# Part of the feed-forward weights prepared during the mixers, through DRAM scratch

## The chip, the cores and the metric

The kernel runs on one core of a Trainium2 chip. The metric is device time in microseconds. The core has five engines that run side by side, each in its own order: TensorE (PE in the profile, with its weight loads as PEld), VectorE (DVE), ScalarE (ACT), GpSimd (POOL) and SyncE (SP), whose queue (SPq) issues all DMAs here.

## The reference

One inference step of a trunk of two layers over 640 tokens (512 latent, 128 context), width 1024. Each layer normalises and modulates x, projects it once, feeds three token mixers (A: grouped-query attention, B: latent attention, C: a gated DeltaNet scan), merges them behind sigmoid gates, and runs a SwiGLU feed-forward of width 2816:

```python
def trunk_layer(x, cvec, p, ctx, angs):
    ...
    h = rms_norm(x, p['norm1']) * (1 + sc1) + sh1
    mix, new_ctx = mixer_block(h, p, ctx, angs)
    x = x + g1 * mix
    h = rms_norm(x, p['norm2']) * (1 + sc2) + sh2
    x = x + g2 * ((jax.nn.silu(h @ p['w_gate']) * (h @ p['w_up'])) @ p['w_down'])
    return x, new_ctx
```

All weights and inputs are float32.

## The kernel before

**Float32 by parts.** A float32 operand is split into a float16 high part and a float16 low part (`split`: ScalarE writes the high part, VectorE the low part). `mm3` multiplies two such operands with three matmuls per 128 rows of depth: low weight with high input, high with high, high with low input. Weights are split in the kernel, as they come in from DRAM.

**A layer.** `layer` writes the program in this order: input projection, mixer C's short convolution and triangular solve, mixer A's projections and attention, with the scan of mixer C (`ds` on PE) run step by step between them; then mixer B; then `merge`; then `ffn`. The rest of the input projection (`background`, gates and other columns, PSUM tile `f` from `hh`) has a very low priority and fills PE wherever nothing else is ready; `bgload` converts its weights. The triangular solve is a chain of products `zw` and differences `z` on VectorE; the first scan step needs its end. A scheduler sets each engine's order from priorities and a modelled time line; each engine then runs its list in order.

**The feed-forward.** Gate, up and down products are done with a Strassen-like scheme of 7 products instead of 8 on 2 × 2 quarters. `block` runs the 7 products of one output block. A weight chunk is a 512 KB tile `wf` of 4 quarters. `lhs_parts` turns it into 7 left operands: three quarters are split directly (tiles `wh`, `wl` for the first chunk of a block, `uh`, `ul` for the second), four sums of quarters go into `ls` (three on GpSimd, one on VectorE) and are split into `vh`, `vl`:

```python
            self.split(w[0], w[1], a[:, 1:4], SW)
            tt = lambda i, x, y, op: (nc.gpsimd if i in SUMP else nc.vector).tensor_tensor(t[:, i], x, y, op=op)
            tt(0, a[:, 0], a[:, 3], ALU.add)
            ...
            self.split(v[0], v[1], t, SW)
```

`wf` and `ls` have two buffers each, shared by all chunks in turn.

`gate_up(u)`, u = 0 to 10, runs two blocks (g: gate, up) of two chunks each (c), 44 chunks per layer. ScalarE copies intermediate products out of PSUM (`du2`, `du3`, `dp1`: `du` and `dp` in the profile), VectorE adds, GpSimd multiplies gate and up (`ff_s`). `inputs(u)` then makes the input of the down product: four differences `ts` on GpSimd, split by ScalarE and VectorE into `f`. `down` runs over units 0 to 3 after unit 4's gate and up, over 4 to 7 after unit 8's, and over 8 to 10 at the end; it reads another 24 chunks, 4 of them of half size, so 22 full ones. That makes 66 blocks of weights per layer. During layer 0's feed-forward PE also computes layer 1's modulations (`wm`).

## Time and profile before

| | us |
|---|---|
| median of 3 runs (lowest, highest) | 2723.09 (2721.92, 2725.84) |
| the profiled execution | 2721.82 |
| its span in the trace | 2719.8 |
| layer 0: solve, scan, mixer B | 250 to 338, 338 to 632, 632 to 785 |
| layer 0: feed-forward, gate and up of units 0 to 4, then 5 to 8 | 913 to 1068, 1118 to 1232 |
| layer 1: feed-forward, gate and up of units 0 to 4, then 5 to 8 | 2262 to 2400, 2446 to 2556 |

The stretches are read from the trace by which line PE works for, to a few us. Busy time is the time in which an engine executes; a wait row names the engine and line that waited, what its wait ended with, and the sum, number and longest of these waits. "Clock" is the granted TensorE clock as a share of full speed.

### The profile page before, as it was taken

The page shows a single profiled execution, that of the slowest core. Times are in us where ns is not written, and L with a number is a line of the kernel's source. Part 1 is how long each engine was busy: PE and PEld are TensorE (multiplying, and loading weights), DVE is VectorE, ACT ScalarE, POOL GpSimd, SP SyncE. Part 2 cuts the span into 40 slices and gives each one's busy share as a digit, 9 for nine tenths or more (in the row PEclk, how much of TensorE's full clock was granted, in tenths as well). Part 3 has the DMA queues.
Part 4 walks back from the last instruction along what each step waited for, and adds up shares of the span by engine and source line. Part 5 has one row for each costly group of instructions (what it writes and reads, how often), then busy time and mean ns, then how long its engine had stood idle before and what let it go on. Part 6 is the DMA issues. An engine that isn't in the chain of part 4 may idle for free.

```text
span 2719.8 us, 52951 instructions
## 1 busy us (share of the span) xinstructions
PE 2495.5 (92%) x21022; PEld 1613.9 (59%) x21022; DVE 1810.2 (67%) x2966; ACT 1295.5 (48%) x2466; POOL 1093.1 (40%) x1012
## 2 busy tenths in 40 slices
PE   5999999999998899999889989999989988889896
PEld 3656666566345656656566666665653565656574
DVE  5749854325756778878787497442277657888887
ACT  5532754444642544444465346554545444444444
POOL 3252111111137567565533632011112565766764
PEclk9999999999998999999989999999999999999998
DMA  7787564436434164432243965543462621222222
GB/s 295 225 260 233 151 195 124 126 123 202 114 131 157 61 206 131 162 117 89 73 137 106 264 184 161 163 122 119 126 205 74 210 78 40 78 78 78 78 82 67
DMA packets 249400, 382.50 MB, mean 141 GB/s; under 512 B 109824, under 2 KB 155968, under 8 KB 249152
## 3 DMA queue, kind: packets, MB, share of 16 engines
q1 hardware_dynamic: 249152, 379.12, 45.0%
q8 instruction: 165, 2.70, 0.4%
q14 instruction: 83, 0.68, 0.1%
HBM read 291.30 MB, written 73.92 MB: 134 GB/s over the span
## 4 chain that ended last, share of the span: by engine, by line
PE 44%; DVE 18%; POOL 14%; DMA 12%; issue 5%; ACT 5%; SPq 2%; DVEq 0%; POOLq 0%; ACTq 0%
PE f L195 12%; PE g L195 8%; POOL ls L1210 8%; PE ao L872 5%; PE s L195 5%; DMA wf<-in_w_gu 3%; POOL ts L1191 3%; DMA wf<-in_w_down 2%; DVE wl L183 2%; POOL ff_s L1307 1%; DVE vl L189 1%; DVE wl L189 1%; DVE ul L189 1%; DVE z L671 1%; ACT wh L188 1%
## 5 line engine op out<-in xcount | busy, mean ns | idle before, releaser
L195 PEld LDWEIGHTS <-wh 128*128 128x128 f16 x5760 | 560.1, 99 | 250.8 <-issue 34.8
L195 PEld LDWEIGHTS <-wl 128*128 128x128 f16 x2880 | 285.6, 99 | 176.9 <-issue 70.8
L195 PE MATMUL s<-xs,vh 128*128 128x320 f16 x1408 | 308.2, 302 | 25.3 <-ACT du L213 10.7
L195 PEld LDWEIGHTS <-vh 128*128 128x128 f16 x2112 | 209.9, 100 | 92.1 <-issue 5.3
L195 PE MATMUL f<-hh,wh 128*128 128x320 f16 x896 | 251.1, 302 | 1.7 <-ACT st L213 1.6
L195 PE MATMUL f<-hh,wl 128*128 128x320 f16 x896 | 251.2, 301 | 0.0
L1210 POOL TENSOR_TENSOR ls<-wf 128x256 f32<-128x256 f32 (+1 forms) x136 | 137.3, 1014 | 203.7 <-DVE vl L189 188.4
L875 POOL TENSOR_TENSOR pacc<-pe,pacc 128x512 f32<-128x512 f32 x64 | 84.2, 1315 | 325.7 <-ACT pe L213 315.5
L195 PE MATMUL s<-xs,vl 128*128 128x320 f16 x704 | 203.9, 302 | 0.2 <-DVE vl L189 0.2
L195 PE MATMUL g<-hh,wh 128*128 128x320 f16 x704 | 198.7, 304 | 2.8 <-ACT sq L213 1.5
L195 PE MATMUL g<-hh,wl 128*128 128x320 f16 x704 | 198.4, 304 | 0.0
L189 DVE SCALAR_TENSOR_TENSOR vl<-ls,vh 128x1024 f16<-128x1024 f32 (+1 forms) x136 | 185.7, 1389 | 10.8 <-ACT vh L188 10.8
L329 DVE SCALAR_TENSOR_TENSOR wl<-wf,wh 128x512 f16<-128x512 f32 x130 | 89.1, 713 | 137.2 <-ACT wh L213 136.8
L195 PE MATMUL s<-f,vh 128*128 128x320 f16 x704 | 159.9, 310 | 17.1 <-ACT du L213 9.3
L195 PEld LDWEIGHTS <-vl 128*128 128x128 f16 x1056 | 104.8, 99 | 95.8 <-issue 49.2
L183 DVE SCALAR_TENSOR_TENSOR wl<-wf,wh 128x1024 f16<-128x1024 f32 (+4 forms) x116 | 132.6, 1157 | 33.3 <-ACT wh L182 33.0
L188 ACT ACTIVATE vh<-ls 128x1024 f16<-128x1024 f32 (+1 forms) x136 | 133.8, 1020 | 39.4 <-POOL ls L1210 39.3
L195 PE MATMUL f<-hl,wh 128*128 128x320 f16 x896 | 148.7, 299 | 0.0
L195 PE MATMUL s<-xs,wh 128*128 128x320 f16 x528 | 133.6, 306 | 10.0 <-ACT du L213 10.0
L814 POOL TENSOR_TENSOR rc<-rc,rot 128x512 f32<-128x512 f32 (+1 forms) x16 | 27.6, 1724 | 283.3 <-DVE rc L813 266.9
L182 ACT ACTIVATE wh<-wf 128x1024 f16<-128x1024 f32 (+4 forms) x116 | 95.2, 832 | 92.3 <-PE g L195 72.9
L195 PE MATMUL s<-xs,uh 128*128 128x320 f16 x528 | 134.4, 305 | 4.2 <-ACT uh L188 4.2
(382 smaller groups left out, 6202.1 us busy)
## 6 DMA issues: line engine op xcount, KB each, us to landing
wm<-in_w_mod SPq DMA_DIRECT2D x96, 512.0 KB, 4.6
wf<-in_w_gu SPq DMA_DIRECT2D x88, 512.0 KB, 3.6
wf<-in_w_in SPq DMA_DIRECT2D x112, 256.0 KB, 3.5
wf<-in_w_in SPq DMA_DIRECT2D x44, 512.0 KB, 4.0
wf<-in_w_down SPq DMA_DIRECT2D x40, 512.0 KB, 3.6
d_s<-sd SPq DMA_DIRECT2D x20, 768.0 KB, 5.4
d_gate<-st SPq DMA_DIRECT2D x96, 160.0 KB, 3.1
sd<-d_s SPq DMA_DIRECT2D x20, 768.0 KB, 5.7
```

The costliest lines, as they stand in the source:

```text
L182: nc.scalar.activation(wh, wf, AF.Copy, scale=SW)
L183: nc.vector.scalar_tensor_tensor(wl, wf, SW, wh, op0=ALU.mult, op1=ALU.subtract)
L188: nc.scalar.activation(hi, src, AF.Copy, scale=scale)
L189: nc.vector.scalar_tensor_tensor(lo, src, scale, hi, op0=ALU.mult, op1=ALU.subtract)
L195: mm = lambda *a, **k: nc.tensor.matmul(out, *a, skip_group_check=more, **k)
L329: nc.vector.scalar_tensor_tensor(wl[:, sl], wf, SW, wh[:, sl], op0=ALU.mult, op1=ALU.subtract)
L671: nc.vector.tensor_tensor(z[a, j + 1:N, 0:cc], z[a, j + 1:N, 0:cc], wj, op=ALU.subtract)
L814: nc.gpsimd.tensor_tensor(w[:n], w[:n], self.rot[:n, NS:], op=ALU.mult)
L872: nc.tensor.matmul(po[64 * j:64 * j + 64, :], vt(h, kt), es[j], start=n == 0, stop=n == 4)
L875: nc.gpsimd.tensor_tensor(acc[1], es[1], acc[1], op=ALU.add)
L1191: sub = lambda i, x, y: (self.nc.gpsimd if i in pool else self.nc.vector).tensor_tensor(out[:, i], x, y, op=ALU.subtract)
L1210: tt = lambda i, x, y, op: (nc.gpsimd if i in SUMP else nc.vector).tensor_tensor(t[:, i], x, y, op=op)
```

## The change

Eighteen chunks per layer are converted before the feed-forward: the second chunk (c = 1) of both blocks of units 1 to 5 while mixer A runs, and of units 6 to 9 while mixer B runs. `prepare` loads each in two halves of 256 KB (`pf`), makes the sums (`pt`) and the split parts (`pp`), and stores the half's 7 + 7 parts in a scratch tile in DRAM, `d_pw`, 448 KB per half. All this has a priority below the background projection, and one buffer of each tile. In the feed-forward, `lhs` takes such a chunk with one load of 896 KB and no work on any other engine. Other chunks go as before, but all 14 parts of a chunk now lie in one tile `pw` with five buffers, in place of `wh`/`wl`, `uh`/`ul` and `vh`/`vl`. The weights are laid out in another order in DRAM, so that halves of a chunk are contiguous. `wh` and `wl` of the other weights move to a pool that is closed before the feed-forward.

```diff
+AT7 = {1: 0, 2: 1, 4: 2, 5: 3, 6: 4, 7: 5, 3: 6}
+PWB = 5
+READY = ([(u, g, 1) for u in range(1, 6) for g in range(2)], [(u, g, 1) for u in range(6, 10) for g in range(2)])
...
-        self.wp = pool("wst", 3)
+        self.wp = pool("wst", 2)
...
-        wh = self.sb(pool or self.wp, [128, n], "wh", F16)
-        wl = self.sb(pool or self.wp, [128, n], "wl", F16)
+        wh = self.sb(pool or self.wq, [128, n], "wh", F16)
+        wl = self.sb(pool or self.wq, [128, n], "wl", F16)
...
-    def lhs_parts(self, pool, src, n, c):
-
-        nc = self.nc
-        wide = lambda p, tag, dt, bufs: self.sb(p, [128, 1024], tag, dt, bufs)[:, :4 * n].rearrange("p (q n) -> p q n", q=4)
+    def lhs_parts(self, out, a, t):
+        nc = self.nc
+        self.split(out[:, :, 0, 0:3], out[:, :, 1, 0:3], a[:, :, 1:4], SW)
+        tt = lambda i, x, y, op: (nc.gpsimd if i in SUMP else nc.vector).tensor_tensor(t[:, :, i], x, y, op=op)
+        tt(0, a[:, :, 0], a[:, :, 3], ALU.add)
+        tt(1, t[:, :, 0], a[:, :, 1], ALU.subtract)
+        tt(2, a[:, :, 1], a[:, :, 0], ALU.subtract)
+        tt(3, a[:, :, 2], t[:, :, 1], ALU.subtract)
+        self.split(out[:, :, 0, 3:7], out[:, :, 1, 3:7], t, SW)
+    def lhs(self, pool, src, n, ready=None):
+        nc = self.nc
+        tile = lambda p, tag, bufs, dt=F32, q=4: self.sb(p, [128, q * 256], tag, dt, bufs)[:, :q * 128 * n]
         with self.tc.high_priority():
-            a, t = wide(self.wp, "wf", F32, 2), wide(pool, "ls", F32, 2)
-            nc.sync.dma_start(a, src)
-            if c % 2:
-                w = [self.sb(pool, [128, 768], tag, F16, 2)[:, :3 * n].rearrange("p (q n) -> p q n", q=3) for tag in ("uh", "ul")]
-            else:
-                w = [wide(self.wp, tag, F16, None)[:, 1:4] for tag in ("wh", "wl")]
-            v = [wide(pool, tag, F16, 4) for tag in ("vh", "vl")]
-            self.split(w[0], w[1], a[:, 1:4], SW)
-            tt = lambda i, x, y, op: (nc.gpsimd if i in SUMP else nc.vector).tensor_tensor(t[:, i], x, y, op=op)
-            tt(0, a[:, 0], a[:, 3], ALU.add)
-            tt(1, t[:, 0], a[:, 1], ALU.subtract)
-            tt(2, a[:, 1], a[:, 0], ALU.subtract)
-            tt(3, a[:, 2], t[:, 1], ALU.subtract)
-            self.split(v[0], v[1], t, SW)
-        pick = lambda x, q: [x[i][:, q] for i in range(2)]
-        return {1: pick(w, 0), 2: pick(w, 1), 4: pick(w, 2), 5: pick(v, 0), 6: pick(v, 1), 7: pick(v, 2), 3: pick(v, 3)}
+            out = tile(pool, "pw", PWB, F16, 14)
+            if ready is not None:
+                nc.sync.dma_start(out, ready)
+            out = out.rearrange("p (n i q c) -> p n i q c", n=n, i=2, q=7)
+            if ready is None:
+                quads = lambda x: x.rearrange("p (n q c) -> p n q c", n=n, q=4)
+                a, t = tile(self.wp, "wf", 2), tile(pool, "ls", 2)
+                nc.sync.dma_start(a, src)
+                self.lhs_parts(out, quads(a), quads(t))
+        return {q: [[out[:, k, i, j] for k in range(n)] for i in range(2)] for q, j in AT7.items()}
+    def prepare(self, l, pool, parts):
+        nc = self.nc
+        with self.tc.high_priority(-2 * 10 ** 6):
+            for u, g, c in parts:
+                d = self.d_pw[u, g, c] = self.sb(self.dp, [128, 2, 14 * 128], f"d_pw{l}{u}{g}{c}", F16)
+                for k in range(2):
+                    a, t = self.sb(pool, [128, 1, 4, 128], "pf"), self.sb(pool, [128, 1, 4, 128], "pt")
+                    o = self.sb(pool, [128, 1, 2, 7, 128], "pp", F16)
+                    nc.sync.dma_start(a.rearrange("p n q c -> p (n q c)"), self.a["w_gu"][l, u, g, c, :, 512 * k:512 * k + 512])
+                    self.lhs_parts(o, a, t)
+                    nc.sync.dma_start(d[:, k], o.rearrange("p n i q c -> p (n i q c)"))
...
-                self.mm3(bank, lambda k, i: w[q][i][:, 128 * k:128 * k + 128], lambda k, i: rhs(q, i, k0 + k), n,
+                self.mm3(bank, lambda k, i: w[q][i][k], lambda k, i: rhs(q, i, k0 + k), n,
...
-                chunks = [(self.lhs_parts(wp, self.a["w_gu"][l, u, g, c], 256, c), 2 * c, 2) for c in range(2)]
+                chunks = []
+                for c in range(2):
+                    ready = self.d_pw.get((u, g, c))
+                    if ready is not None:
+                        ready = ready.rearrange("p k x -> p (k x)")
+                    chunks.append((self.lhs(wp, self.a["w_gu"][l, u, g, c], 2, ready), 2 * c, 2))
...
-                    src = self.a["w_down"][l, m // 2][:, 512 * u:512 * (u + n)].rearrange("p (q n) -> p q n", q=4)
-                    chunks.append((self.lhs_parts(wp, src, 128 * n, len(chunks)), u, n))
+                    chunks.append((self.lhs(wp, self.a["w_down"][l, m // 2][:, 512 * u:512 * (u + n)], n), u, n))
...
+        self.d_pw = {}
+        self.wq = self.pool(ws, f"wst{l}", 3)
...
+            self.prepare(l, self.pool(e1, f"pa{l}"), READY[0])
...
+            self.prepare(l, self.pool(es, f"pb{l}"), READY[1])
...
-    r["w_gu"] = quads(gu).reshape(L, NF // 2, 2, 2, 128, 4, 256)
+    r["w_gu"] = quads(gu).swapaxes(-3, -2).reshape(L, NF // 2, 2, 2, 128, 1024)
```

GpSimd, one unit of gate and up in layer 1's feed-forward. `ff_s` is gate times up, `ts` the differences for the down product, `ls` the weight sums. Before:

```order
L1307 TENSOR_TENSOR ff_s<-ff_s,ff_o 128x320 x2
L1191 TENSOR_TENSOR ts<-ff_s 128x320 x2
L1191 TENSOR_TENSOR ts<-ff_s,ts 128x320
L1210 TENSOR_TENSOR ls<-wf 128x256 x2
L1191 TENSOR_TENSOR ts<-ff_s,ts 128x320
L1210 TENSOR_TENSOR ls<-ls,wf 128x256 x2
L1307 TENSOR_TENSOR ff_s<-ff_s,ff_o 128x320
L1210 TENSOR_TENSOR ls<-wf,ls 128x256 x2
L1210 TENSOR_TENSOR ls<-wf 128x256
L1210 TENSOR_TENSOR ls<-ls,wf 128x256
L1210 TENSOR_TENSOR ls<-wf 128x256
L1210 TENSOR_TENSOR ls<-wf,ls 128x256
```

After:

```order
L1331 TENSOR_TENSOR ff_s<-ff_s,ff_o 128x320 x2
L1196 TENSOR_TENSOR ts<-ff_s 128x320 x2
L1196 TENSOR_TENSOR ts<-ff_s,ts 128x320
L1207 TENSOR_TENSOR ls<-wf 128x2x128
L1196 TENSOR_TENSOR ts<-ff_s,ts 128x320
L1207 TENSOR_TENSOR ls<-ls,wf 128x2x128
L1207 TENSOR_TENSOR ls<-wf,ls 128x2x128
L1331 TENSOR_TENSOR ff_s<-ff_s,ff_o 128x320
L1207 TENSOR_TENSOR ls<-wf 128x2x128
L1207 TENSOR_TENSOR ls<-ls,wf 128x2x128
L1207 TENSOR_TENSOR ls<-wf,ls 128x2x128
```

Before, twelve `ls` of a unit (two more follow the rows shown) stand between one group of `ff_s` and the next; after, six.

VectorE at the end of layer 0's triangular solve (`zw`, `z`), with mixer A's rotation (`rc`, `aq`) between. `pf`, `pt` and `pp` are the tiles of `prepare`. Before:

```order
L669 TENSOR_TENSOR zw<-lt,z 64x87
L813 STREAM_SHUFFLE rc<-aq 128x512
L671 TENSOR_TENSOR z<-z,zw 64x3x29
L815 TENSOR_TENSOR aq<-aq,rot 128x512
L669 TENSOR_TENSOR zw<-lt,z 64x60
L671 TENSOR_TENSOR z<-z,zw 64x2x30
L669 TENSOR_TENSOR zw<-lt,z 64x31
L816 TENSOR_TENSOR aq<-aq,rc 128x512
L671 TENSOR_TENSOR z<-z,zw 64x31
```

After:

```order
L1207 TENSOR_TENSOR pt<-pf 128x128
L674 TENSOR_TENSOR zw<-lt,z 64x87
L194 SCALAR_TENSOR_TENSOR aql<-aq,aqh 128x640
L676 TENSOR_TENSOR z<-z,zw 64x3x29
L194 SCALAR_TENSOR_TENSOR pp<-pf,pp 128x384
L674 TENSOR_TENSOR zw<-lt,z 64x60
L194 SCALAR_TENSOR_TENSOR pp<-pt,pp 128x512
L676 TENSOR_TENSOR z<-z,zw 64x2x30
L188 SCALAR_TENSOR_TENSOR wl<-wf,wh 128x256
L674 TENSOR_TENSOR zw<-lt,z 64x31
L676 TENSOR_TENSOR z<-z,zw 64x31
```

Rows of `prepare` now stand between the last steps of the chain. From the first `zw` to the last `z` of this layer VectorE has 266 rows before and 332 after, 36 of them of `prepare`: 12 of the 20 halves of this stretch.

PE after the last scan step of layer 0 (`ds`). `f` from `hh` is the background projection; `f` and `ao` from `yh` is the next branch's output projection. Before:

```order
L759 MATMUL ds<-sd,S 64x64 x2
L761 MATMUL ds<-sd,sw 64x64 x2
L195 LDWEIGHTS wl
L195 MATMUL f<-hh,wl 128x320
L195 LDWEIGHTS wh
L195 MATMUL f<-hh,wh 128x320
```

After:

```order
L764 MATMUL ds<-sd,S 64x64 x2
L766 MATMUL ds<-sd,sw 64x64 x2
L200 LDWEIGHTS wh
L200 MATMUL f<-yh_5056,wh 128x320
L200 LDWEIGHTS wh
L200 MATMUL ao<-yh_5056,wh 128x320
L200 LDWEIGHTS wl
L200 MATMUL f<-yh_5056,wl 128x320
```

Before, 187 matmuls of the background projection stand behind the last `ds` matmul (205 in layer 1); after, none.

## Rows read from the trace of the kernel before

**Rows 1.** Page, part 1: busy us (share of span) and instructions of each engine.

```profile
PE 2495.5 (92%) x21022; PEld 1613.9 (59%) x21022; DVE 1810.2 (67%) x2966; ACT 1295.5 (48%) x2466; POOL 1093.1 (40%) x1012
```

**Rows 2.** Stretches: length, PE, PEld, DVE, ACT, POOL busy, clock, DMA share, GB/s.

```profile
250.00:338.00 88.00, 81.14 (x795) 57.61 (x794) 82.21 (x202) 56.20 (x108) 15.30 (x17) 1.00 0.58 160
338.00:632.00 294.00, 291.11 (x3440) 186.94 (x3439) 109.74 (x178) 146.63 (x311) 39.75 (x32) 1.00 0.47 138
632.00:785.00 153.00, 146.53 (x741) 65.79 (x741) 99.68 (x176) 80.99 (x173) 28.93 (x21) 1.00 0.44 133
913.00:1068.00 155.00, 141.84 (x1101) 87.91 (x1101) 117.34 (x163) 69.65 (x117) 95.49 (x97) 0.98 0.50 167
...
1118.00:1232.00 114.00, 105.22 (x800) 67.95 (x798) 88.56 (x115) 49.38 (x81) 72.67 (x70) 0.97 0.42 144
...
2262.00:2400.00 138.00, 122.59 (x828) 82.74 (x828) 107.88 (x135) 63.43 (x103) 92.03 (x85) 0.95 0.21 66
...
2446.00:2556.00 110.00, 97.25 (x691) 67.56 (x690) 89.06 (x108) 50.26 (x83) 75.71 (x72) 0.98 0.25 79
...
2608.00:2656.00 48.00, 46.05 (x339) 32.83 (x337) 39.07 (x54) 24.09 (x38) 30.46 (x30) 1.00 0.27 78
```

**Rows 3.** PE waits (us, times, longest): 913:1068, 1118:1232, 2262:2400, 2446:2556, 2262:2705 in turn.

```profile
PE s L195 <- ACT du L213: 4.5, 2, 2.4
...
PE s L195 <- ACT du L213: 4.4, 3, 2.5
...
PE s L195 <- DVE ul L189: 1.8, 1, 1.8
...
PE s L195 <- ACT du L213: 7.7, 6, 2.0
PE s L195 <- ACT uh L188: 4.0, 2, 2.1
...
PE s L195 <- DVE ul L189: 1.6, 4, 0.5
...
PE s L195 <- DVE ul L189: 4.8, 3, 1.8
PE s L195 <- ACT du L213: 3.8, 3, 1.8
PE s L195 <- DVE ff_s L1236: 3.6, 3, 1.4
...
PE s L195 <- DVE ul L189: 10.7, 11, 3.2
PE s L195 <- ACT uh L188: 6.2, 5, 2.1
```

**Rows 4.** Waits of GpSimd and ScalarE, 2262 to 2400.

```profile
POOL ls L1210 <- DVE vl L189: 28.4, 5, 6.7
...
ACT f L188 <- POOL ts L1191: 26.6, 8, 5.7
```

**Rows 5.** Chain that ended last, 2465 to 2535: start us, us, what.

```profile
2473.25 3.65 DMA wf<-in_w_gu
...
2501.56 3.61 DMA wf<-in_w_gu
```

**Rows 6.** Conversion operations: count, ns min/median/max, first and last start, forms.

```profile
L1210 DVE TENSOR_TENSOR ls<-wf x136: 412/943/1082, 831.2 to 2690.6; 128x256 f32<-128x256 f32 x128, 128x128 f32<-128x128 f32 x8
...
L1210 POOL TENSOR_TENSOR ls<-wf,ls x136: 584/790/1704, 836.1 to 2691.6; 128x256 f32<-128x256 f32 x128, 128x128 f32<-128x128 f32 x8
...
L189 DVE SCALAR_TENSOR_TENSOR vl<-ls,vh x136: 678/1219/1892, 838.6 to 2695.5; 128x1024 f16<-128x1024 f32 x128, 128x512 f16<-128x512 f32 x8
...
L189 DVE SCALAR_TENSOR_TENSOR ul<-wf,uh x68: 551/951/1608, 839.9 to 2689.1; 128x768 f16<-128x768 f32 x60, 128x384 f16<-128x384 f32 x8
```

**Rows 7.** The attention's running sum on VectorE, same columns.

```profile
L874 DVE TENSOR_TENSOR pacc<-pe,pacc x64: 678/692/1645, 464.8 to 2120.4; 128x512 f32<-128x512 f32 x64
```

**Rows 8.** DMA issues: count, KB each, median us to landing.

```profile
sd<-d_s SPq DMA_DIRECT2D x20, 768.0 KB, 5.7
```

More of the change, by code (lines that the diff above doesn't have):

```diff
@@ L1418, in layer @@
         tc = self.tc
-        ys = ExitStack()
+        ys, ws = ExitStack(), ExitStack()
         self.yh, self.yl = [], []
+        self.d_pw = {}
+        self.wq = self.pool(ws, f"wst{l}", 3)
         def branch(b):
@@ L1511, in layer @@
                 self.branch_out(l, 2, bgp)
+        ws.close()
         wr = self.pool(ys, f"wr{l}", 4, "right")
@@ L1577, in layout @@
     quads = lambda w: np.stack([w[..., 1, 0, :, :], w[..., 0, 0, :, :], w[..., 0, 1, :, :], w[..., 1, 1, :, :]], -3)
-    r["w_gu"] = quads(gu).reshape(L, NF // 2, 2, 2, 128, 4, 256)
+    r["w_gu"] = quads(gu).swapaxes(-3, -2).reshape(L, NF // 2, 2, 2, 128, 1024)
     dn = f("w_down").reshape(L, 2, NF // 2, 128, 4, 2, 128).transpose(0, 4, 3, 5, 1, 2, 6)
-    dn = quads(dn)
-    r["w_down"] = cat([dn[..., u:u + 2, :].reshape(L, 4, 128, -1) for u in range(0, NF // 2, 2)], -1)
+    r["w_down"] = quads(dn).swapaxes(-3, -2).reshape(L, 4, 128, -1)
     return {k: np.ascontiguousarray(v) for k, v in r.items()}
```

## Prediction

> **What bounds the kernel now.** I read the engines' busy time first [rows 1]. TensorE (PE) is busy 92% of the span of 2719.8 us, so no change can bring much unless it gives PE back some of the other 8%. The next view is the table of stretches [rows 2]. Its columns are length, then busy time of PE, weight loads, VectorE, ScalarE and GpSimd, then the granted clock. While layer 0's DeltaNet scan runs (338 to 632), PE is busy 291.11 of 294 us. In mixer B (632 to 785) it is busy 146.53 of 153. In the gate and up parts of the feed-forward it is busy less: 141.84 of 155 and 105.22 of 114 in layer 0, 122.59 of 138 and 97.25 of 110 in layer 1. This is where the lost time is.
>
> Matmul counts say the same. The stretch 2608 to 2656 is fully fed at clock 1.00: 46.05 us for 339 matmuls, or 0.136 us each [rows 2]. The 828 matmuls of 2262 to 2400 would need 112.6 us at that price and take 138. The 691 of 2446 to 2556 would need 94 and take 110.
>
> Why PE waits there is in its waits [rows 3]. Some end on `ul` and `uh`, the low and high halves of the second weight chunk of a block. More end on `du`, a copy from PSUM by ScalarE. That copy is short, so it is late because of what stands in front of it. On ScalarE that is `f`, which waited 26.6 us in this stretch for `ts`, GpSimd's sums [rows 4]. On GpSimd the sums `ls` of the weight chunks waited 28.4 us for `vl`, the split that frees the `ls` buffer [rows 4]. GpSimd runs in order, so `ts` stands behind those `ls`. A ring of load, split, sum, split and next load thus runs through four engines. The chain of what ended last shows its period: two of its load steps, one unit of gate and up apart, start 28.31 us from each other [rows 5]. A unit has 168 matmuls (7 products, 3 matmuls per k, 4 k, 2 blocks), or 22.8 us at 0.136. **The conversion ring, not PE, sets the pace of gate and up.**
>
> **Removed from the feed-forward.** In units 1 to 9 of each layer the second chunk of both blocks arrives converted: 18 of 44 chunks. Each takes with it the `ul` split (0.95 us median), the fourth sum (0.94) and the `vl` split (1.22) on VectorE, 3.1 us together, and three sums of about 0.79, 2.4 us, on GpSimd [rows 6]. A unit keeps two of four conversions, so the ring's part of the period falls from 28.3 to about half, 14 to 15 us, well under PE's 22.8. The sums' order on GpSimd shows it: six `ls` per unit instead of twelve around the same `ts`.
>
> What PE gets back, for both layers:
> - `ul` and `uh` in the gate and up stretches: 1.8 + 1.6 + 4.8 + 4.0 = 12.2 us [rows 3]. These tiles belong to the chunk that is now ready. I take 12.
> - `du`, with the two sums that wait behind it: 4.5 + 4.4 + 7.7 + 3.8 + 3.6 = 24.0 us [rows 3]. `ts` still comes from GpSimd, still waits for the gate and up values, and units 0 and 10 change nothing. I take 15, bounds 6 and 22.
> - The clock. The granted clock was 0.98, 0.97, 0.95 and 0.98 in those four stretches [rows 2], a loss of 3.1 + 3.4 + 6.9 + 2.2 = 15.6 us. It stood at 1.00 where PE had no gaps. Fewer gaps should bring about half back: 7, bounds 0 and 12.
> - The down stretches convert everything as before, but enter with five weight buffers and a ring that is no longer behind. Layer 1's whole feed-forward shows 10.7 + 6.2 us on `ul` and `uh`, of which 1.6 + 4.8 + 4.0 are counted above; 6.5 are left [rows 3], and for both layers at most twice that. I take 5, bounds 0 and 13.
>
> Sum: 12 + 15 + 7 + 5 = **39 us**.
>
> **Added in the mixers.** Each of the 18 chunks is done in two halves, 36 per layer. A half costs VectorE at least 0.551 + 0.412 + 0.678 = 1.64 us: the minima in these rows are the half-size forms [rows 6]. It costs GpSimd three sums, by the nearest row at least 0.58 each, 1.75 us. It also adds a 256 KB load and a 448 KB store on SP's queue. 20 halves lie in mixer A's part, 33 us of VectorE; 16 in mixer B's, 26 us.
>
> Mixer A's part has two stretches. In the scan VectorE is busy 109.74 of 294 us [rows 2], so whatever runs there is hidden. In the triangular solve ahead of it (250 to 338) it is busy 82.21 of 88, and the z chain sets the end. The order puts 36 of VectorE's preparation rows, 12 halves, ahead of the last `z`: 12 × 1.64 = 20 us where 6 are free. The scan then starts some 14 to 20 us later. What hides this is filler. The background input projection had 187 matmuls left on PE after the last scan step, and now has none. 187 × 0.136 = 25 us [rows 2], more than the delay. So this costs about nothing, and 20 us per layer if the cover fails.
>
> In mixer B, VectorE goes from 99.68 to about 126 of 153 us, 82%. Stretches with such a VectorE exist: it is busy 107.88 of 138 and 89.06 of 110 in the feed-forward, and PE idles 11% there against 4% in mixer B [rows 2]. Seven per cent of 153 is 11 us. I take half, because nothing in the mixer waits for a prepared half except the next half: **5 us per layer, 10 in all**, bounds 0 and 31 per layer (11 + 20).
>
> GpSimd is busy 28.93 of 153 us there and gains 48 sums, 28 us. One operation of VectorE can take far longer than another of the same size: the sum `pacc` took 692 ns median and 1645 at worst there [rows 7], and GpSimd does the other half of that sum. The Trainium skill, "SBUF — State Buffer", section "Who interferes with whom", speaks against this part of the change: a GpSimd operation and a VectorE operation with two SBUF inputs take one port pair as an exclusive lock. The 1645 ns agree with it, though no run here isolates it. By it, the 48 sums could hold VectorE for up to their 28 us per mixer B, which would bring it to 154 of 153 us there and the sum above from 10 us to over 50.
>
> **Transfers.** A ready chunk is read as 896 KB instead of 512. The nearest row, 768 KB out of scratch, took 5.7 us [rows 8]; my estimate by size is 896/768 × 5.7 = 6.7 us. PE takes 42 × 0.136 = 5.7 us per chunk, but the ready chunk is followed by one of 512 KB and five buffers stand ahead. I take 1 us. SP's queue issues the loads of ready chunks in turn with the others and waits only for a free buffer. The stores stand on the same queue in the mixers; each waits for its half's last split, and the loads of background weights behind it wait along. That is inside the 5 us per layer.
>
> Net: 39 − 10 − 1 = 28 us. The new layout keeps the number of elements of every sum and split, so I cost it at nothing. The profiled execution took 2721.82 us, 2.0 more than its span and 1.3 less than the median of the three runs. 2721.8 − 28 is 2694; on the median's side 2695. I say **2694**.
>
> **Rivals.**
> - *The `du` chain stays.* `ts` → `f` → `du` may run late for its own reason: `ts` waits for values that PE itself makes late in the unit. Then only the 12 us, a little clock and down come back, 12 + 6 + 3 = 21, less 11, is 10: about **2712**. For it: `ts` remains on GpSimd. Against it: the 28.4 us of `ls` waits stand directly ahead of `ts` [rows 4].
> - *PE fully fed.* All bounds at their best and mixers free: 12 + 22 + 12 + 13 = 59, so **2663**. For it: a ring of 15 us beside PE's 22.8 leaves 8 us of slack per unit. Against it: the first and last units and the norms keep their waits.
> - *Slower: VectorE becomes the bound in the mixers.* The place is the solve and mixer B. If operations there stretch as the slowest `pacc` did (1645 ns for 692, [rows 7]), VectorE has no idle time left, and the 20 us of the solve and the 26 of mixer B come out in full: 46 per layer, 92 in all. Less 39, the time is about **2775**; with the filler covering the solve's part, 2735. It decides from the point where the delay of the scan exceeds 25 us of filler and VectorE passes its 53 idle us in mixer B. For it: 82.21 of 88. Against it: 126 of 153 is still below the end.
> - *The change doesn't do what it says.* If the ready chunk came too late from scratch, nothing would be gained. The order puts all stores into the scratch of a layer in the mixers, before its feed-forward begins, so I give this nothing.
>
> **How the numbers follow.** Forecast (2680 to 2705): 0.42. The `du` chain stays (2705 to 2717): 0.20. Well fed (below 2680): 0.17. Within 0.2% of the time before, which is about what a measurement of this kernel can tell (2717.6 to 2728.5): 0.10. Slower, mostly the VectorE rival: 0.11. So faster 0.79, same 0.10, slower 0.11. For 8 in 10 the range leaves out the far end of each side: low 2667 (gains of 55 with the mixers free), high 2721 (gains of 19 with little `du` back, mixers 9 per layer).
>
> **What would show it.** Right: no PE waits on `ul` or `uh` in units 1 to 9; GpSimd's waits on `vl` well below 28.4; `du` waits below half; one unit of layer 1 in about 23 to 25 us instead of 28.3; the granted clock there near 1.00; PE in the scan and in mixer B as busy as before. Wrong: the same `du` and `f` waits; PE waiting on weights from scratch; a scan that begins over 25 us later with PE idle behind it; `pacc` and rotation sums on VectorE at their maxima through mixer B.

## The result: slower, although the feed-forward gained twice what was forecast

The changed kernel takes 2756.73 us (median of 4 runs, 2752.04 to 2760.37) against 2723.8: a ratio of 1.012, 95% interval 1.0102 to 1.0137. Forecast were 2694, between 2667 and 2721. The profiled execution took 2760.37 us and its span is 2758.5, so 38.7 us longer than the profiled span of before.

To find where the time went I cut both traces at two events per layer: the first matmul of gate and up (`s<-xs`) and the last matmul of down (`s<-f`). What lies between them is the feed-forward; all else of a layer is "mixers" here.

| us, profiled executions | before | after | |
|---|---|---|---|
| layer 0: mixers | 913.7 | 977.9 | +64 |
| layer 0: feed-forward | 468.6 | 435.5 | −33 |
| layer 1: mixers | 869.5 | 925.2 | +56 |
| layer 1: feed-forward | 453.6 | 405.5 | −48 |

So the feed-forwards gave 81 us, where the prediction summed 39, and the mixers took 120, where it priced 10.

**The feed-forward of after.** Four stretches of gate and up, from four tables of stretches (columns as in [rows 2]):

```profile
978.00:1115.00 137.00, 133.38 (x1047) 82.44 (x1045) 80.70 (x130) 53.75 (x94) 61.87 (x67) 0.98 0.59 208
...
1179.00:1270.00 91.00, 91.00 (x702) 61.52 (x700) 53.96 (x80) 36.44 (x62) 42.77 (x43) 1.00 0.51 170
...
2339.00:2458.00 119.00, 112.46 (x816) 79.75 (x814) 80.30 (x121) 53.37 (x96) 62.10 (x67) 0.99 0.29 98
...
2516.00:2599.00 83.00, 82.75 (x610) 59.40 (x609) 50.75 (x73) 35.55 (x61) 43.77 (x43) 1.00 0.39 123
```

In [rows 2] the second and fourth kind of stretch had PE busy 105.22 of 114 and 97.25 of 110 us at clocks of 0.97 and 0.98. Here PE is busy 91.00 of 91 and 82.75 of 83 at 1.00. PE's waits in layer 1's whole feed-forward, then ScalarE's and GpSimd's in 2339 to 2458:

```profile
PE s L200 <- DVE pw L194: 7.7, 6, 2.4
PE s L200 <- ACT xs L218: 4.5, 2, 3.2
PE s L200 <- ACT f L193: 2.1, 1, 2.1
...
ACT f L193 <- POOL ts L1196: 13.9, 8, 3.9
...
POOL ls L1207 <- DMA wf<-in_w_down: 6.4, 2, 6.2
```

No row for `du` is left in layer 1 (0.2 us in layer 0). GpSimd no longer waits for the split that frees `ls` (28.4 us in [rows 4]), and `f` waits 13.9 us for `ts` instead of 26.6. In the chain that ended last, one piece in layer 1 is PE alone:

```profile
2486.26 98.44 PE s L200 x711
```

In these stretches the ring no longer sets the pace; PE does. In the last of them 610 matmuls take 83 us, or 22.9 us for the 168 of a unit, where the prediction's mark was 23 to 25.

**The mixers of after.** First the stretch from the first to the last operation of the triangular solve in layer 0, of before (215 to 336) and of after (217 to 391):

```profile
215.00:336.00 121.00, 112.37 (x1064) 79.06 (x1063) 114.03 (x273) 63.76 (x123) 27.37 (x24) 1.00 0.66 191
```

```profile
217.00:391.00 174.00, 149.32 (x1267) 100.31 (x1265) 152.86 (x342) 90.64 (x184) 71.33 (x62) 0.95 0.65 199
```

The solve takes 174 us instead of 121; in layer 1 it takes 167 instead of 125. VectorE is busy 94% of it before, and 88% after, over a longer stretch. Its groups there in after (line, operation, shapes, count, then busy us and mean ns, then idle before):

```profile
L674 DVE TENSOR_TENSOR zw<-lt,z 128x60 f32<-128x60 f32 (+23 forms) x92 | 37.2, 415 | 0.7
L676 DVE TENSOR_TENSOR z<-z,zw 128x31 f32<-128x31 f32 (+30 forms) x93 | 35.7, 395 | 0.6
...
L194 DVE SCALAR_TENSOR_TENSOR pp<-pt,pp 128x512 f16<-128x512 f32 x12 | 8.1, 678 | 6.3 <-ACT pp L193 6.3
L334 DVE SCALAR_TENSOR_TENSOR wl<-wf,wh 128x512 f16<-128x512 f32 x10 | 8.1, 812 | 0.1
L194 DVE SCALAR_TENSOR_TENSOR pp<-pf,pp 128x384 f16<-128x384 f32 x12 | 6.5, 543 | 1.1 <-ACT pp L193 1.1
L833 DVE TENSOR_REDUCE amxa<-ao 128x1 f32<-128x512 f32 x9 | 6.1, 676 | 0.4 <-PE ao L832 0.4
...
L1207 DVE TENSOR_TENSOR pt<-pf 128x128 f32<-128x128 f32 x12 | 3.9, 322 | 5.0 <-DMA pf<-in_w_gu 5.0
...
L820 DVE TENSOR_TENSOR aq<-aq,rot 128x512 f32<-128x512 f32 x3 | 3.0, 993 | 0.0
...
L667 DVE COPY lt<-z 64x1024 f32<-64x1024 f32 (+1 forms) x2 | 2.1, 1038 | 3.6 <-DMA z<-d_b 3.6
```

The 12 halves are there: `pp`, `pp` and `pt` take 8.1 + 6.5 + 3.9 = 18.5 us, close to the 20 of the prediction. But VectorE's busy time rose by 152.86 − 114.03 = 38.8. The other 20 us are work of mixer A (`amxa`, more `wl` of background weights, the rotation `aq` of two more heads) that stood behind the last `z` before. Mixer A's own path did not wait for the solve, so as the solve got longer, that work came in front of its end. And VectorE now idles 21 us there instead of 7, most of it with a row of `prepare` first in its order: 6.3 + 1.1 for ScalarE's half of `pp`, 5.0 for the load of `pf`; 3.6 are the solve's own load. The solve's operations themselves take 37.2 + 35.7 us of the 174. 18.5 + 20 + 14 is the 53 us.

PE waited in this stretch for those engines, and the granted clock fell from 1.00 to 0.95:

```profile
PE dl L249 <- POOL csa L1018: 9.4, 1, 9.4
PE dl L574 <- DVE cs L555: 8.4, 3, 3.8
```

The scan then ends at 667 us instead of 602, 65 later: 55 lie at the last `z`, the other 10 in the scan itself. Before, 36 us of other work lay between its end and the first matmul of mixer B; after, 1.3. So the filler took up 34 us of the delay, and 31 us came out.

**Mixer B.** From its first to its last branch projection, before and after:

```profile
637.00:840.00 203.00, 194.38 (x1086) 100.37 (x1087) 145.41 (x234) 102.26 (x203) 64.69 (x50) 0.99 0.52 165
```

```profile
668.00:910.00 242.00, 212.76 (x1140) 106.66 (x1141) 184.41 (x297) 128.15 (x253) 102.69 (x106) 0.96 0.61 199
```

39 us more, and VectorE's busy time grew by 39.0. That the two are equal does not show that one is the other: PE's busy time grew by 18.4 us and its idle time by 20.6. Some 54 small projection matmuls, 7 us, ran as filler of mixer A before and now stand in mixer B, and the granted clock is 0.96 instead of 0.99. With these 39 us, the 31 before them and a merge that is 5 to 6 us shorter, the 64 us of layer 0 are complete.

### The profile page after: what moved, and what is told of

Same layout as the page of the kernel before. It is cut to its first block, busy times and chain, and to the rows that moved or that the text cites. A ratio compares the mean times of both kernels' runs of the same rounds, so it can differ in the third digit from the quotient of the medians.

```text
span 2758.5 us, 53585 instructions
## 1 busy us (share of the span) xinstructions
PE 2522.0 (91%) x21022; PEld 1615.0 (59%) x21022; DVE 1777.5 (64%) x3074; ACT 1309.1 (47%) x2538; POOL 1091.2 (40%) x1120
## 4 chain that ended last, share of the span: by engine, by line
PE 48%; DVE 18%; DMA 14%; POOL 7%; issue 6%; ACT 5%; SPq 2%; DVEq 0%; ACTq 0%; POOLq 0%
PE s L200 18%; PE f L200 8%; PE g L200 6%; PE ao L877 4%; DMA pf<-in_w_gu 3%; DMA d_pw<-pp 2%; POOL pt L1207 2%; DVE pw L194 1%; DVE wl L188 1%; POOL ls L1207 1%; DMA wf<-in_w_gu 1%; DVE z L676 1%; DVE pp L194 1%; POOL ts L1196 1%; DVE zw L674 1%
## 5 line engine op out<-in xcount | busy, mean ns | idle before, releaser
L200 PEld LDWEIGHTS <-pw 128*128 128x128 f16 x5544 | 540.7, 99 | 274.3 <-issue 39.7
L200 PEld LDWEIGHTS <-wh 128*128 128x128 f16 x4944 | 480.8, 99 | 225.4 <-issue 39.6
L200 PE MATMUL s<-xs,pw 128*128 128x320 f16 x3696 | 524.1, 301 | 11.2 <-ACT xs L218 7.3
L200 PE MATMUL s<-f,pw 128*128 128x320 f16 x1848 | 269.9, 302 | 19.7 <-DVE pw L194 11.2
L1207 POOL TENSOR_TENSOR ls<-wf 128x256 f32<-128x256 f32 x100 | 95.6, 956 | 231.6 <-DMA wf<-in_w_gu 124.8
L194 DVE SCALAR_TENSOR_TENSOR pw<-ls,pw 128x1024 f16<-128x1024 f32 x100 | 138.4, 1384 | 0.8 <-ACT pw L193 0.8
L1331 POOL TENSOR_TENSOR ff_s<-ff_s,ff_o 128x320 f32<-128x320 f32 x60 | 66.6, 1110 | 128.5 <-DVE ff_o L1260 121.3
L218 ACT ACTIVATE du<-s 128x320 f32<-128x320 f32 x136 | 58.0, 428 | 123.2 <-PE s L200 123.2
L200 PE MATMUL g<-hl,wh 128*128 128x320 f16 x704 | 116.4, 303 | 0.0
L193 ACT ACTIVATE pw<-ls 128x1024 f16<-128x1024 f32 x100 | 101.1, 1011 | 28.9 <-POOL ls L1207 27.2
```

Source lines behind the costliest of these rows:

```text
L193: nc.scalar.activation(hi, src, AF.Copy, scale=scale)
L194: nc.vector.scalar_tensor_tensor(lo, src, scale, hi, op0=ALU.mult, op1=ALU.subtract)
L200: mm = lambda *a, **k: nc.tensor.matmul(out, *a, skip_group_check=more, **k)
L218: i = self.nc.scalar.activation(out, in_, func, scale=scale, **kw)
L1331: (nc.gpsimd if u < NH - 1 and i != 2 else nc.vector).tensor_tensor(c, c, o, op=ALU.mult)
```

## Experiments

The last two columns sum both layers, divided as above, and are of one profiled execution each. The ratio compares runs of the kernel with runs of before on the same chip, and the time that the text gives for a whole run is the median of its runs. Runs of one kernel spread over 4 to 19 us (late_a: 2698 to 2718), and a profile can lie off the median (c_no_dve 9 us below, b_only 7 above), so a difference of under some 10 us in these columns is not sure.

| run | what is in it | ratio to before (95%) | mixers | feed-forwards |
|---|---|---|---|---|
| before | | 1 | 1783 | 922 |
| after | | 1.012 (1.0102 to 1.0137) | 1903 | 841 |
| no_ready | buffers, pools and layout only | 0.9902 (0.9873 to 0.9931) | 1799 | 885 |
| nr_pwb3 | the same, `pw` 3 deep | 1.0315 (1.0299 to 1.0331) | 1785 | 1010 |
| nr_pwb4ls3 | `pw` 4, `ls` 3 deep | 1.0087 (1.0071 to 1.0103) | 1802 | 930 |
| prep_only | prepared, not used | 1.0281 (1.0253 to 1.0308) | 1900 | 881 |
| use_only | used, one chunk prepared | 0.9807 (0.9787 to 0.9828) | 1818 | 841 |
| dma_only | its loads and stores | 0.9887 (0.9868 to 0.9906) | 1839 | 842 |
| compute_only | its splits and sums | 0.9999 (0.9987 to 1.0012) | 1869 | 843 |
| c_no_dve | the same without VectorE's | 0.9906 (0.9877 to 0.9934) | 1837 | 840 |
| c_no_pool | the same without GpSimd's | 0.9888 (0.9855 to 0.992) | 1840 | 841 |
| a_only | mixer A's ten chunks | 1.0117 (1.0089 to 1.0144) | 1878 | 860 |
| a_all | all 18 in mixer A | 1.0132 (1.0106 to 1.0158) | 1902 | 845 |
| late_a | ten, after the solve | 0.9924 (0.9901 to 0.9947) | 1822 | 861 |
| late_ab | after, ten of it late | 1.0025 (1.0009 to 1.0041) | 1877 | 845 |
| b_only | mixer B's eight chunks | 0.9976 (0.996 to 0.9992) | 1845 | 865 |
| late_all | all 18, after the solve | 1.0143 (1.012 to 1.0166) | 1907 | 842 |

### Gain and cost apart

prep_only looks up no ready chunk; use_only prepares one chunk per layer and reads it 18 times; no_ready prepares none.

```diff
-                    ready = self.d_pw.get((u, g, c))
+                    ready = None
```

```diff
             for u, g, c in parts:
+                if (u, g, c) != READY[0][0]:
+                    self.d_pw[u, g, c] = self.d_pw[READY[0][0]]
+                    continue
```

```diff
+READY = ([], [])
```

> All 36 chunks are prepared and stored, but the feed-forward converts every chunk itself, as before; only the tile pw with five buffers and the new layout stay. The trace of after has the mixers and merges 120 us longer than before (64 in layer 0, 56 in layer 1) and the two feed-forwards 81 us shorter (33 and 48). Theory 'the ready chunks make the whole gain': the feed-forwards take again 469 + 454 us as before, so 2724 + 117 = about 2840. Rival 'the five pw buffers make part of the gain': feed-forwards of about 880 us in sum, so about 2800.

> Only one chunk per layer is prepared, and all 18 ready loads of a layer read that one (the other chunks' products are therefore not the reference's). It prices the feed-forward's gain with the mixers nearly free. If the 81 us stand by themselves: 2724 - 81 + about 4 for two chunks = 2645 (2635 to 2660). Rival 'the gain comes from chunks of the next stages that were begun earlier, in the longer mixers and merge': over 2670.

> Nothing is prepared; the new layout, the tile pw with five buffers and the moved weight pools stay. prep_only had feed-forwards of 453 + 429 us, 41 less than before, and use_only had mixers and merges 35 us longer than before though only one chunk per layer was prepared. Theory 'the buffers alone bring 41 us and the pools cost nothing': 2724 - 41 = 2683. Rival 'the moved pools cost the mixers the 35 us of use_only': about 2715.

prep_only took 2801 us, its rival's number: the mixers are 1900, as in after, so the preparation costs the same whether it is used or not. Its feed-forwards are 881 and no_ready's 885, against 922. **Half of the feed-forward's gain, 37 to 41 us, comes from what no_ready keeps (five buffers of `pw`, the layout, the moved pools), and the other 40 to 44 from the ready chunks.** use_only, at 2676, has its rival's number but not for the rival's reason: the feed-forwards keep the whole gain (841 us) with the mixers nearly free, and it is the mixers that still take 35 us more than before. no_ready shows 16 of these without any preparation. In its mixer B VectorE has nine splits into `pw` for the first chunks of the feed-forward (13 us), where before had two (`ul` and `vl`, 3 us); its two mixers B are 13 and 9 us longer, the merges behind them some 5 shorter. The other 19 in use_only, for one chunk per layer, I did not resolve; its solves take 128 and 133 us against 121 and 124 in no_ready. no_ready, at 2700.4, lies between its two as well and is faster than both kernels.

### Why the feed-forward gains without any preparation

```diff
-PWB = 5
+PWB = 3
```

```diff
-PWB = 5
+PWB = 4
...
-                a, t = tile(self.wp, "wf", 2), tile(pool, "ls", 2)
+                a, t = tile(self.wp, "wf", 2), tile(pool, "ls", 3)
```

Both start from no_ready.

> As no_ready (2700.4 us, feed-forwards 453 + 432 us against 469 + 454 of before), but pw has three buffers instead of five. Theory 'depth': the 37 us of the feed-forwards come from conversions that may run five chunks ahead; with three they are lost, feed-forwards 910 us or more, 2720 to 2745. Rival 'layout': they come from the shorter sums of the new layout (the median of VectorE's sum ls is 0.68 us against 0.94); then the depth matters little: 2698 to 2708.

> As no_ready, but pw with four buffers and ls with three instead of two: can a version without any preparation be better than no_ready? If ls is what closes the ring (GpSimd's ls waits 40 us for VectorE's split in no_ready, 188 in before): 2685 to 2698. If the depth of pw counts for more: 2702 to 2715.

nr_pwb3 took 2812 us and nr_pwb4ls3 2749, each worse than either of its numbers: feed-forwards of 1010 us with three buffers, 930 with four, 885 with five. Before has four buffers of `vh` and `vl`, and its 922 us lie next to the 930. So it is the depth. The layout's shorter sums did not hold it up. With three buffers PE waits for high parts that are converted late (PE's waits in layer 0's feed-forward of nr_pwb3):

```profile
PE s L200 <- ACT pw L193: 28.5, 48, 2.5
PE s L200 <- ACT du L218: 23.2, 37, 3.0
```

A third `ls` does not make up for a fifth `pw`. What five buffers do to the ring shows in the idle time before the operations on `ls` (the sums, most of them on GpSimd, and the splits of the sums), whole span, of before and of no_ready:

```profile
L1210 DVE TENSOR_TENSOR ls<-wf x136: 412/943/1082, 831.2 to 2690.6; 128x256 f32<-128x256 f32 x128, 128x128 f32<-128x128 f32 x8
...
  DVE vl L189: 188.4, 35
...
  DMA wf<-in_w_gu: 1.8, 4
```

```profile
L1207 DVE TENSOR_TENSOR ls<-wf x136: 277/683/1114, 813.1 to 2671.2; 128x256 f32<-128x256 f32 x128, 128x128 f32<-128x128 f32 x8
...
  DMA wf<-in_w_gu: 129.2, 53
...
  DVE pw L194: 40.2, 6
```

The wait for the split that frees `ls` falls from 188 to 40 us. It is not all gained: before the same operations the engines now idle 129 us for loads of `wf`, where before they idled 1.8. What makes those loads late was not tried.

### Which part of the preparation costs

dma_only keeps the loads and stores and stores a constant tile; GpSimd writes one column of that tile per half. compute_only works on one loaded half per mixer and stores only the last chunk. c_no_dve and c_no_pool are compute_only with the named engine's work left out of all chunks but the last of each mixer.

```diff
...
-                    self.lhs_parts(o, a, t)
+                    nc.gpsimd.memset(o[:, 0, 0, 0, 0:1], 0.01)
...
```

```diff
...
-                    nc.sync.dma_start(d[:, k], o.rearrange("p n i q c -> p (n i q c)"))
+                    if (u, g, c) == parts[-1]:
+                        nc.sync.dma_start(d[:, k], o.rearrange("p n i q c -> p (n i q c)"))
```

> All loads (256 KB) and stores (448 KB) of the preparation stand on the queue, but no split and no sum is done; the stores come from a constant tile, GpSimd writes one column of it per half. Theory 'head of line': the loss in the mixers is time in which a preparation's split or sum stands first in the order of VectorE, ScalarE or GpSimd and waits for its own load or store; without these the mixers are within 20 us of before, so about 2645 to 2665. Rival 'queue and traffic': SP's queue and the added 25 MB per layer delay the loads of the mixers; then the loss stays, 2740 or more. Rival 'volume' (the added work itself): as head of line, 2645 to 2665.

> All splits and sums of the preparation are done, on one loaded half per mixer, and only the last chunk is stored (the other chunks' products are not the reference's). No split waits for a load or a store. Theory 'head of line': VectorE's and ScalarE's waits on the preparation's DMAs (in the trace of after 52 us of VectorE for pf, 84 us of ScalarE for the store d_pw, 24 for pf, both layers) are gone and most of the 117 us with them: 2660 to 2690. Rival 'volume': VectorE's 59 us and GpSimd's share per layer cost as much without the waits: 2730 to 2760. Rival 'queue and traffic': 2650.

> As compute_only, but of all chunks but the last of each mixer only ScalarE's splits and GpSimd's three sums are done; VectorE's part (low halves and the fourth sum) is left out. compute_only took 2725.6, use_only 2675.6. Theory 'VectorE's added time': 2680 to 2690, mixer B near use_only's 211 and 218 us. Rival 'GpSimd's sums hold VectorE': 2710 to 2726, mixer B near compute_only's 244 us. In between, both.

> As compute_only, but of all chunks but the last of each mixer GpSimd's three sums are left out; VectorE's and ScalarE's part is done. Against no_ready, mixer A's part (background to the end of its tail) took 485 and 548 us, compute_only 494 and 554 with 61 and 213 matmuls fewer in it, c_no_dve 508 and 564; mixer B took 216 and 216, compute_only 245 and 243, c_no_dve 216 and 215. Theory 'VectorE in mixer B, GpSimd in mixer A': mixer B again 235 to 245, mixer A's part within 8 us of no_ready, about 2705. Rival 'VectorE alone does not matter, only VectorE beside GpSimd on one port': mixer B near 216 to 222 and the time near 2685.

No theory had its way alone. Against no_ready's 1799 the mixers cost 40 us with the transfers alone, 70 with the splits and sums alone, 104 with both. "Head of line" (waits of a split for its own load or store) falls as the main cause: compute_only has no such waits and still loses most. "Queue and traffic" is real but the smaller part. compute_only took 2726 us; leaving out VectorE's work (2702) saves 23 of them, leaving out GpSimd's (2697) saves 28, where the profiled mixers say 32 and 29.

The place tells more than the sum. The length of layer 0's triangular solve, first to last operation, and of mixer B in both layers:

| us | before | no_ready | dma_only | c_no_dve | c_no_pool | compute_only | after |
|---|---|---|---|---|---|---|---|
| solve | 121 | 121 | 131 | 132 | 162 | 176 | 174 |
| mixer B | 203 | 216 | 222 | 216 | 234 | 245 | 242 |
| mixer B, layer 1 | 207 | 216 | 222 | 215 | 248 | 244 | 246 |

Both follow VectorE's part. The solve gets longer by 10 us with the transfers, by 11 with ScalarE and GpSimd, by 41 with VectorE and ScalarE. compute_only is no better than after in the solve, with 19 halves in it, not 12; no load or store paces it there. Mixer B is as long without VectorE's part as with no preparation at all. The stretches of layer 0's mixer B, of no_ready, c_no_dve and compute_only:

```profile
639.00:855.00 216.00, 198.53 (x1088) 101.03 (x1089) 155.50 (x242) 107.30 (x209) 73.28 (x59) 0.98 0.52 162
```

```profile
664.00:880.00 216.00, 194.62 (x1066) 98.26 (x1064) 156.82 (x248) 119.57 (x237) 98.65 (x106) 0.98 0.54 168
```

```profile
647.00:892.00 245.00, 213.93 (x1154) 107.36 (x1151) 186.99 (x295) 128.01 (x252) 104.67 (x107) 0.95 0.50 155
```

GpSimd's 25 us more (98.65 against 73.28) cost nothing without VectorE's part. With VectorE's 31 us more (186.99 against 155.50) mixer B is 29 us longer, of which 66 matmuls that moved in from mixer A are 9. But compute_only has a longer solve as well, so these 29 us are not yet VectorE's work in mixer B alone.

### Where the preparation stands

late_a lets the first half of a layer wait for `xf`, which is made from the last part of the solve. late_ab is the changed kernel with that edit, late_all has all 18 chunks in mixer A with it.

```diff
+                    if k == 0 and (u, g, c) == parts[0]:
+                        self.act(a[:, 0, 0, 0:1], self.xf[4][:, 0, 0, 0:1], AF.Copy)
                     nc.sync.dma_start(a.rearrange("p n q c -> p (n q c)"), self.a["w_gu"][l, u, g, c, :, 512 * k:512 * k + 512])
```

```diff
-            self.prepare(l, self.pool(e1, f"pa{l}"), READY[0])
+            pa = self.pool(e1, f"pa{l}")
...
                     st = self.a_proj(l, ap, self.pool(e3, f"at{l}", 2, "right"), tick)
+                self.prepare(l, pa, READY[0])
```

a_only, a_all and b_only change the lists in `READY` alone.

> The ten chunks of mixer A are prepared and used, the eight of mixer B are converted in the feed-forward. Theory 'mixer B pays for VectorE's and GpSimd's added volume, mixer A has room': the feed-forwards are about 22 us shorter than without any ready chunk, mixer A's part is 0 to 20 us longer per layer, mixer B as in use_only: 2690 to 2715. Rival 'each prepared half costs the same wherever it is done' (81 us between use_only and after for 34 halves per layer, so 20 of 36 cost 45 us): 2735.

> All 18 chunks are prepared in mixer A's part, none in mixer B. VectorE is busy 110 of 294 us in the scan of before, so 36 halves of 1.5 to 1.9 us would fit. Theory 'mixer A has room': mixer B as in use_only, mixer A's part 10 to 30 us longer per layer, feed-forwards 841 us: 2690 to 2725. Rival 'same cost wherever': 2757 as after.

> As a_only (2757 us), but the first half of a layer's preparation waits, by a copy of one column, for the tile xf of the last chunk pair, which is made after the triangular solve; so all halves lie in the scan. Theory 'the solve is where mixer A loses' (PE waited 8 to 9 us each on csa from GpSimd and cs from VectorE there): mixer A's part 15 to 25 us per layer shorter than in a_only: 2710 to 2730. Rival 'the scan's own steps are slowed': 2745 to 2760.

> The changed kernel whole (ten chunks in mixer A, eight in mixer B, all used), with one edit: the first half of mixer A's preparation waits for the tile xf of the last chunk pair, after the triangular solve. Theory 'the solve is the step that failed': 53 us of a_only's time went with that edit (2757 to 2704), so 2757 - 53 = about 2704. Rival 'mixer A and mixer B fail together (VectorE has no room in either)': 2725 or more.

> Only the eight chunks of mixer B are prepared and used; mixer A is left alone. Feed-forwards as no_ready less 8/18 of the 44 us between no_ready and after, so 20 us shorter. Theory 'mixer B pays VectorE's added time': mixer B 15 to 26 us per layer longer than no_ready's 216, the time 2710 to 2732. Rival 'mixer B's loss in after came from what mixer A pushed into it': mixer B below 222, the time 2680 to 2690.

> All 18 chunks are prepared in the scan of mixer A, after the solve, none in mixer B. late_a (10 chunks) lengthened mixer A's part by about 10 us per layer; feed-forwards take 20 us less than in late_a. If the scan has room for 36 halves at the same price each (8 us more per layer): 2704 - 20 + 16 = about 2700. If it has not, the tail of filler behind the scan goes to zero and the time is 2720 or more.

a_only refuted my theory of that moment, that mixer A has room: with ten of 18 chunks it is as slow as after (2757 us), and a_all with all 18 there takes 2762. late_a then decided between the two places in mixer A. One dependency, with the call of `prepare` moved behind mixer A's projections, the same work, and 2757 becomes 2704 us. The solve is back to what it was (215 to 336, layer 0 of late_a):

```profile
215.00:336.00 121.00, 112.20 (x1055) 78.79 (x1054) 114.05 (x272) 63.83 (x123) 27.48 (x24) 0.99 0.66 191
```

Behind the scan 34 us of other work are left again. So the collision with the solve costs a_only 53 us. The scan itself takes these 20 halves for less: it is 14 and 15 us longer than no_ready's, and the mixers 23 in sum.

late_ab does not return to 2704: it takes 2734, its rival's number. In the changed kernel whole, the same edit gives back 23 us (2757 to 2734), not 53. Against late_a, mixer B's eight chunks cost mixers of 1877 against 1822 and save 16 us. b_only has them alone: against no_ready it pays 46 us in the mixers for 20 in the feed-forward, and by medians it is 20 us slower (2720 against 2700). So the preparation in mixer B costs more than it saves, whether mixer A prepares or not.

But that is not VectorE's busy time coming out as such. Mixer B of layer 0 and of layer 1, first of b_only, then of a_only, which prepares nothing there:

```profile
642.70:882.30 239.60, 204.64 (x1090) 102.51 (x1091) 180.40 (x291) 121.57 (x240) 101.58 (x105) 0.96 0.61 193
2001.50:2224.40 222.90, 196.79 (x1076) 100.31 (x1075) 183.25 (x290) 119.72 (x237) 104.25 (x105) 0.96 0.65 207
```

```profile
672.00:905.60 233.60, 208.39 (x1139) 105.73 (x1138) 157.92 (x249) 113.10 (x220) 77.55 (x61) 0.97 0.49 157
2027.40:2257.10 229.70, 206.82 (x1139) 105.67 (x1140) 158.73 (x249) 113.19 (x220) 77.55 (x61) 0.98 0.51 159
```

no_ready takes 216 us in both, with VectorE busy 155.50 (shown above) and, in layer 1, 154.16:

```profile
1968.40:2184.40 216.00, 197.10 (x1083) 100.63 (x1082) 154.16 (x241) 105.77 (x207) 73.35 (x59) 0.98 0.52 163
```

In b_only VectorE's 25 and 29 us more go with 24 us in layer 0 and 7 in layer 1. In a_only VectorE has only 2 and 5 us more, and mixer B is still 18 and 14 us longer, with over 50 matmuls more in it that stand ahead of mixer B in no_ready. late_a, with the same ten chunks behind the solve, has 220 and 214 us, so these 18 and 14 came from the longer solve. late_ab has 240 and 224 us where after has 242 and 246, so in layer 1 most of after's loss in mixer B came from mixer A, and in layer 0 hardly any. Why the layers differ (the scan of b_only's layer 1 is also 8 us longer, although nothing is prepared in it) I did not resolve.

late_all (2765 us) seems to have failed for another reason than VectorE's load. A half takes 7 us from load to store with one buffer of each tile, so 36 need 250 us, and the last was stored at 713 us, where mixer B had begun at 671. Its stretch until then:

```profile
671.00:715.00 44.00, 30.53 (x175) 19.00 (x175) 28.69 (x52) 15.44 (x29) 16.12 (x19) 0.81 0.74 262
```

PE is busy 30.53 of 44 us, at a clock of 0.81. That the pool's memory is what mixer B waits for is my reading; it was not tried.

No version that prepares every chunk it reads beat no_ready; late_a's interval overlaps that of no_ready.

## Why the prediction was wrong

- **What bounded the kernel**: right that the conversions and not PE set the pace of gate and up. But no_ready converts all 44 chunks on the same engines and its feed-forwards are 37 us shorter, so half of what was gained hung on how many converted chunks may stand ready and not on the work in the ring.
- **The feed-forward's terms**: right in sign, too small. `ul` and `uh`: 12 taken, and 1.1 us on `pw` are left in the four stretches. `du` and the sums: 15 of 24 taken, all gone. Clock: 7 of 15.6 taken; about 4 are left (2% of 137 us, 1% of 119), so 12 came. That makes 47. The remaining 34 of the 81 us lie in the down stretches and the many idle times that no row of [rows 3] carried, for which I took 5 with a bound of 13. And the sum had one cause where there are two: the five buffers, costed at nothing but for that term, bring half.
- **Added in the mixers**: here the prediction failed. It took 10 us for both layers, nothing in the solve and 5 in each mixer B, and 120 were measured. Both terms were wrong.
- **The solve**: the first step that failed. The count (12 halves) and the price (18.5 us measured for 20) held, but the delay was 53 us, not 14 to 20. The order named 66 more rows ahead of the last `z`, and I priced the 36 of `prepare`; the other 30 cost another 20 us, and VectorE's waits 14. The cover failed with it: 36 us of filler were there, more than the 25 I took, and they hide a delay of 20, not one of 65. I had written the condition down in the rival (a delay of the scan above the filler), with a chance of 0.11. Taking the work out of the solve gave back 53 us in a_only and 23 in the changed kernel.
- **The scan**: "busy 109.74 of 294, so whatever runs there is hidden" did not hold whole: in late_a 20 halves, 33 us of VectorE by my price, make it 14 and 15 us longer.
- **Mixer B**: the second step that failed. It was priced at 5 us per layer from the idle share of other stretches; it took 39 and 39. In no_ready it is already 13 and 9 longer, which the sum did not have. The eight chunks alone (b_only) add 24 and 7, and a_only shows 18 and 14 without any of them, from what the longer solve pushed out of mixer A. Neither 82% busy nor VectorE's added time prices this: in layer 1 of b_only VectorE is busy 183.25 of 222.90 us at a cost of 7.
- **GpSimd against VectorE**: from the rule of the Trainium skill, "SBUF — State Buffer", section "Who interferes with whom", the prediction worked out an estimate of up to 28 us per mixer B for which GpSimd's sums would hold VectorE. That time did not come: c_no_dve has all of the sums, and its mixer B is as long as no_ready's. Single sums of VectorE do get slow beside GpSimd's, which agrees with the rule, but they add 2.7 us there (last section). I had also read [rows 7] wrongly: the 1645 ns stand at 465 us, in mixer A. In mixer B of before no `pacc` of VectorE took over 693 ns.
- **Transfers into the feed-forward**: 1 us taken. PE waited 0.2 us for `pw<-d_pw` in 2516 to 2599, and such a load took 4.5 us (median) where my estimate was 6.7. The transfers of the preparation, put "inside the 5 us", cost the mixers about 20 us per layer (dma_only).
- **The rivals**: the slower one named the right two places, but that its price (46 us per layer) is near the 52 by which the mixers of no_ready and after differ is partly luck. Its 20 and 26 us were VectorE's work coming out in full, with operations as slow as the slowest `pacc`. In the solve the work cost its plain price, and two thirds of the delay were other rows and waits, part of which the filler hid. In mixer B VectorE's 39 us more stayed under the 58 that it had idle in that stretch (203 less 145.41), so it had not become the bound there.

## What to carry to other kernels

An engine with a low mean load can still own a chain of small dependent steps; work of low priority that lands in that chain costs its own time, the time of what the schedule brings forward with it, and its waits. Count all rows that newly stand ahead of the chain's end, not only the added ones. A busy share does not price added work: about as much work of VectorE cost 24 us in one layer's mixer B and 7 in the other's. Where a change brings a deeper buffer along with its main idea, run the buffer alone: here it was worth nearly as much in the feed-forward as the idea, at 16 us in the mixers and not 120.

## What the runs showed of the hardware

A GpSimd sum of 128x128 elements, 0.56 us median, took 5.08 us once in the solve of after. The next one of the same half took 0.46 (GpSimd's timeline: start us, us, then the operation and, in brackets, the idle time before it):

```profile
291.33 5.08 POOL L1207 TENSOR_TENSOR pt<-pf 128x128 f32<-128x128 f32 x1 [3.68 <-DMA pf<-in_w_gu]
296.49 0.46 POOL L1207 TENSOR_TENSOR pt<-pt,pf 128x128 f32<-128x128 f32 x1
```

VectorE worked without a pause in those 5 us. In late_a, outside the solve, the longest of these sums took 0.99 us. PE's 9.4 us for `csa` came later: in GpSimd's order `csa` stood behind the next half's three sums, which began only after 7.45 us of waiting for `pf`, and it took 3.27 us itself, where the three `csa` of layer 0 took 1.54 to 1.89 us in before:

```profile
304.92 0.56 POOL L1207 TENSOR_TENSOR pt<-pf 128x128 f32<-128x128 f32 x1 [7.45 <-DMA pf<-in_w_gu]
...
308.08 3.27 POOL L1018 TENSOR_TENSOR csa<-sq,csa 128x640 f32<-128x640 f32 x1
```

Such long sums are not new with the change. In layer 1's solve of before, `csa` once took 9.61 us, while VectorE ran without a pause, nearly all of it `zw` and `z`, until 1.4 us before its end:

```profile
1625.95 9.61 POOL L1013 TENSOR_TENSOR csa<-sq,csa 128x640 f32<-128x640 f32 x1 [2.65 <-ACT sq L213]
```

It goes the other way too. VectorE's 16 `pacc` sums in layer 0's mixer B (ns, shortest, median and longest, of before, c_no_pool and c_no_dve):

```profile
L874 DVE TENSOR_TENSOR pacc<-pe,pacc x16: 678/686/693, 689.7 to 780.8; 128x512 f32<-128x512 f32 x16
```

```profile
L879 DVE TENSOR_TENSOR pacc<-pe,pacc x16: 673/680/693, 703.4 to 804.0; 128x512 f32<-128x512 f32 x16
```

```profile
L879 DVE TENSOR_TENSOR pacc<-pe,pacc x16: 675/692/1777, 724.9 to 813.4; 128x512 f32<-128x512 f32 x16
```

With GpSimd's added sums and without VectorE's work (c_no_dve) three of the 16 took 1.30 to 1.78 us, each beside a sum of GpSimd that had begun before it; all 16 together took 2.7 us more than before. Without GpSimd's sums (c_no_pool) none is slow in this layer, and one in layer 1 (1.75 us, beside another GpSimd operation that had begun before it). So GpSimd and VectorE each have slow sums beside the other's, while the median stays. That the two hold each other up is the natural reading; no run isolates what they share.
